# A state-space scan on one core: phase tables made on VectorE alone, and transposes of u grouped by row count

## The chip, the core and the metric

The kernel runs as one program on one core of a Trainium2 chip. Five engines work side by side, each through its own list of instructions in order: TensorE (PE, with its weight loads as PEld), VectorE (DVE), ScalarE (ACT), GpSimd (POOL) and SyncE (SP). SP, ACT and POOL also issue DMAs; a DMA that has to wait holds up whatever stands behind it on the engine that issues it. The metric is the device time of one execution in microseconds, as the median of several.

## The reference

One layer of a hybrid backbone over 2048 latent tokens and 256 context tokens of width 1024: a combined input projection, a two-dimensional neighbourhood attention (8 heads), a bidirectional diagonal state-space scan (32 groups of 16 channels, 64 complex states each), a gated merge of the two branches, and a SwiGLU feed-forward network. The part at hand is the scan:

```python
def diag_scan(lb_re, lb_im, bu_re, bu_im):
    a_re = jnp.broadcast_to(lb_re, (1, L) + lb_re.shape)
    a_im = jnp.broadcast_to(lb_im, (1, L) + lb_im.shape)
    return lax.associative_scan(_linear_combine, (a_re, a_im, bu_re, bu_im), axis=1)
...
ur, ui = drive(u_ctx)                       # context scan first
_, _, hc_re, hc_im = diag_scan(lb_re, lb_im, ur, ui)
ur, ui = drive(u_lat)                       # latent scan starts from its final state
```

Every state h obeys h[t] = lam h[t-1] + (B u)[t] with a complex lam, forwards and backwards.

## The kernel before

The kernel cuts the 2304 tokens into 288 chunks of eight. What happens within a chunk is done by matmuls; between chunks the state is multiplied by lam^8. The complex factor is split into its size, r8, and a rotation: the inputs of chunk n are turned back by n times the angle, a real scan with r8 runs over the 288 columns (`tensor_tensor_scan`), and the result is turned forward again. The cosines and sines of n times the angle, n = 0 to 287, are the phase tables `er` and `ei`, 128 x 288 each, one pair of tables for each pair of groups and each direction, 32 in all.

`s5_params` (once, before the scan) makes what the tables are built from: `eb`, the first 32 powers of the rotation for all 32 pairs, and `zz`, the powers 32, 64, 128 and 256. `s5` then runs over four quarters q of the groups, each in two sub-blocks sb, eight sub-blocks in all. A sub-block

- loads u of its four groups into `ut` (three DMAs that POOL issues, L651; the buffer is single), has ACT sort it into `un0`, `un1` (128 chunks each, latent) and `un2` (32 chunks, context) (L652),
- transposes `un` on PE (L658 to L661) into PSUM tiles `pt`, which ACT copies into `ug` (L662). `ug` holds the context columns at both ends, the latent ones between;
- builds `win` and `cl` (DVE, PE, ACT, L684 to L709) and the matrix `mt` (PE, ACT, and 16 DMAs of SP, L719 to L725),
- for each of its two pairs p and two directions d builds the phase tables (L732 to L744), drives the states with PE (`pv`, L750; one PSUM buffer), and runs the scan on DVE (L757 to L772),
- reads out with PE (`py`, L780 to L782), ACT and DVE (L784 to L788).

At the end of a quarter `yn` is transposed (L795) and stored.

The order of the instructions on every engine is set by a scheduler: it plays the program on a timeline of its own and picks the ready instruction with the highest priority. The scan has a higher priority than the input projection `in_proj` of the four token blocks b (three matmuls for each product, L92 to L94, weights through `raw` and split into `whi` by ACT, L70, and `wlo` by DVE, L71), which fills PE between the scan's matmuls. Attention (L884 to L924) follows the scan, again with what is left of `in_proj` beneath it; later the merge. While token block b = 1 is projected, `biases` (L436 to L445) builds the attention's bias tables on POOL: eight heads, each a load, four tensor operations and three stores, in the same POOL list as the loads of u.

Of the kernel before, what the change touches and what calls it, by code (L numbers as in the profile page):

```python
# [10 lines left out]
F32 = mybir.dt.float32  # L11
F32R = mybir.dt.float32r
BF16 = mybir.dt.bfloat16
AF = mybir.ActivationFunctionType
# [38 lines left out]
class Kernel:  # L53
# [394 lines left out]
    def s5_params(self, keep, tmp):  # L448
# [6 lines left out]
        def T(name, *shape):  # L455
            return (keep if name in kept else tmp).tile([P, *shape], F32, name=name)
# [136 lines left out]


        eb = T("eb", 2, 32, n)
        zz = T("zz", 4, 3, n)
        zr, zi = T("zr", n), T("zi", n)
        V.tensor_copy(zr, co[:, 1, :])
        V.tensor_copy(zi, si[:, 1, :])
# [3 lines left out]
        while m <= 256:  # L603
# [6 lines left out]
            if m < 32:  # L610
                for a0 in range(0, m, 8):
                    w = min(8, m - a0)
                    cmul(eb[:, 0, m + a0:m + a0 + w, :], eb[:, 1, m + a0:m + a0 + w, :], eb[:, 0, a0:a0 + w, :], eb[:, 1, a0:a0 + w, :],
                         zr.unsqueeze(1).to_broadcast([P, w, n]), zi.unsqueeze(1).to_broadcast([P, w, n]), (w, n))
            else:
                i = (32, 64, 128, 256).index(m)
                V.tensor_copy(zz[:, i, 0, :], zr)
                V.tensor_copy(zz[:, i, 1, :], zi)
                V.tensor_scalar(zz[:, i, 2, :], zi, -1.0, None, op0=ALU.mult)
            m *= 2  # L620
            if m <= 256:
                cmul(zr, zi, zr, zi, zr, zi, (n,))
# [6 lines left out]
    def s5(self):  # L629
        nc, I = self.nc, self.I  # L630
        V = nc.vector
        with ExitStack() as ctx:
# [7 lines left out]
            for q in range(4):  # L640
                yn = [bp.tile([P, SC, 8, 16], F32, name=f"yn{cb}") for cb in range(2)]
                for sb in range(4 // NQ):
# [10 lines left out]
                        un.append(u)  # L653
                    uc = un[2]
                    ug = bp.tile([P, NG, SEQC + NCC], F32, name="ug")
                    for g in range(NG):
                        pt = psT.tile([P, SEQC + NCC], F32, name="pt")
                        nc.tensor.transpose(pt[:, 0:NCC], uc[:NCC, g], self.ident[:NCC, :NCC])  # L658
                        for cb in range(2):
                            nc.tensor.transpose(pt[:, NCC + cb * P:NCC + cb * P + P], un[cb][:, g], self.ident)  # L660
                        nc.tensor.transpose(pt[:, SEQC:SEQC + NCC], uc[:NCC, g], self.ident[:NCC, :NCC])  # L661
                        nc.scalar.copy(ug[:, g, :], pt)  # L662


                    win = bp.tile([P, 2, NQ, 2, 2, 64], F32, name="win")
# [61 lines left out]
                    for p0 in range(0, NQ, 2):  # L727
                        hst = {}
                        for p in (p0, p0 + 1):
                            for d in range(2):  # L730
                                pr = d * 16 + pr0 + p
                                er = pp.tile([P, SEQC], F32, name="er")  # L732
                                ei = pp.tile([P, SEQC], F32, name="ei")
                                nc.scalar.copy(er[:, 0:32], self.eb[:, 0, :, pr])
                                nc.scalar.copy(ei[:, 0:32], self.eb[:, 1, :, pr])
                                for i, m in enumerate((32, 64, 128, 256)):
                                    w = min(m, SEQC - m)
                                    zr, zi, zn = (self.zz[:, i, x, pr:pr + 1] for x in range(3))
                                    ea = pp.tile([P, P], F32, name="ea", bufs=1)
                                    eb = pp.tile([P, P], F32, name="eb", bufs=1)  # L740
                                    nc.scalar.activation(ea[:, :w], er[:, 0:w], AF.Copy, scale=zr)
                                    nc.scalar.activation(eb[:, :w], ei[:, 0:w], AF.Copy, scale=zr)
                                    V.scalar_tensor_tensor(er[:, m:m + w], ei[:, 0:w], zn, ea[:, :w], op0=ALU.mult, op1=ALU.add)
                                    V.scalar_tensor_tensor(ei[:, m:m + w], er[:, 0:w], zi, eb[:, :w], op0=ALU.mult, op1=ALU.add)  # L744
                                pv = psV.tile([P, 2, 512], F32, name="pv")
                                for ri in range(2):
                                    for g2 in range(2):
# [599 lines left out]
```

## Time and profile before

| | |
|---|---|
| median of 3 runs | 3233.46 us (3233.32 to 3234.92) |
| profiled execution, its own time | 3233.39 us |
| its span, first to last instruction | 3231.6 us |
| granted TensorE clock, mean | 0.987 |
| PE busy | 97% |
| DVE, ACT, POOL busy | 73%, 49%, 28% |

The span is counted from the first instruction; 1.8 us of the execution's time lie outside it. The scan stands between about 140 and 870 us, with `in_proj` beneath it; attention and the merge follow until about 1600 us, then the feed-forward network. PE is busy nearly all the time, so what counts is PE's work, its waits, and the stretches in which its granted clock is at the lower of its two levels (0.5 of full, 1.2 GHz instead of 2.4 GHz).

### The profile page before, as it was taken

How to read it: one execution, taken by the hardware profiler on the slowest of the kernel's cores; microseconds unless marked ns; L12 is line 12 of the kernel's file. 1: busy time of each engine (PE TensorE's matmuls, PEld its weight loads, DVE VectorE, ACT ScalarE, POOL GpSimd, SP SyncE). 2: the span in 40 equal slices, each digit the busy share in tenths (PEclk: the TensorE clock that was granted, in tenths of full speed). 3: DMA queues.
4: the chain of work that ended last, by engine and by line, in shares of the span. 5: the costliest groups of instructions: out<-in, count | busy, mean ns of one | idle time of the engine just before them, and what ended most of it. 6: DMA issues, size and time to landing. Idle time of an engine off the chain costs nothing.

```text
span 3231.6 us, 54283 instructions
## 1 busy us (share of the span) xinstructions
PE 3119.2 (97%) x20600; PEld 2727.7 (84%) x20600; DVE 2348.4 (73%) x4153; ACT 1570.3 (49%) x2746; POOL 898.9 (28%) x856
## 2 busy tenths in 40 slices
PE   7999978999999998999999999999999999999998
PEld 5987766787787778788888988888989898989988
DVE  6689787897753565665657867887858966897766
ACT  4445434454355555555554444445535543554534
POOL 2000052000223232323300544742242423341243
PEclk9999989999999999999999999999999999999999
DMA  8545567454776897987847434434344434443332
GB/s 321 186 125 172 166 194 241 163 163 140 228 211 193 268 259 213 277 238 220 254 130 269 139 126 146 141 131 147 122 136 132 150 111 131 141 147 131 112 111 101
DMA packets 212853, 564.27 MB, mean 175 GB/s; under 512 B 31785, under 2 KB 63657, under 8 KB 212593
## 3 DMA queue, kind: packets, MB, share of 16 engines
q1 hardware_dynamic: 155008, 437.48, 41.2%
q0 software_dynamic: 28032, 87.64, 10.0%
q10 hardware_dynamic: 29552, 35.70, 3.2%
q8 instruction: 162, 2.65, 0.3%
q14 instruction: 99, 0.80, 0.1%
HBM read 446.95 MB, written 111.61 MB: 173 GB/s over the span
## 4 chain that ended last, share of the span: by engine, by line
PE 79%; DVE 9%; DMA 6%; issue 3%; POOL 1%; ACT 1%; SPq 0%; ACTq 0%; DVEq 0%; POOLq 0%
PE ps L92 15%; PE ps L94 15%; PE ps L93 15%; PE ps L1068 8%; PE ps L1066 8%; PE ps L1067 8%; PE o L924 3%; DVE wlo L71 3%; PE w L884 2%; PE w L905 1%; DMA raw<-in_w_qk 1%; PE pv L750 1%; PE c L886 1%; PE c L907 1%; DVE n L1130 1%
## 5 line engine op out<-in xcount | busy, mean ns | idle before, releaser
L71 DVE TENSOR_TENSOR wlo<-raw,whi 128x1024 fp32r<-128x1024 f32 (+1 forms) x522 | 688.0, 1325 | 324.6 <-ACT whi L70 323.1
L70 ACT CAST whi<-raw 128x1024 fp32r<-128x1024 f32 (+1 forms) x522 | 508.3, 976 | 519.6 <-PE ps L94 185.8
L1066 PE MATMUL ps<-X,whi 128*128 128x256 f32 x2464 | 693.4, 284 | 13.2 <-DVE u L1078 8.4
L1068 PE MATMUL ps<-X,wlo 128*128 128x256 f32 x2464 | 692.4, 284 | 11.9 <-DVE wlo L71 11.7
L1067 PE MATMUL ps<-X,whi 128*128 128x256 f32 x2464 | 689.9, 283 | 0.0
L1066 PEld LDWEIGHTS ps<-X,whi 128*128 128x128 f32 x2464 | 471.2, 191 | 17.9 <-DVE u L1078 11.7
L1068 PEld LDWEIGHTS ps<-X,wlo 128*128 128x128 f32 x2464 | 470.5, 191 | 15.1 <-DVE wlo L71 14.9
L1067 PEld LDWEIGHTS ps<-X,whi 128*128 128x128 f32 x2464 | 471.3, 191 | 0.5
L92 PE MATMUL ps<-n,whi 128*128 128x512 f32 (+1 forms) x800 | 318.2, 398 | 10.3 <-ACT t L382 6.7
L93 PE MATMUL ps<-n,whi 128*128 128x512 f32 (+1 forms) x800 | 316.7, 396 | 0.0
L94 PE MATMUL ps<-n,wlo 128*128 128x512 f32 (+1 forms) x800 | 316.3, 396 | 0.5 <-DVE wlo L71 0.5
L92 PE MATMUL ps<-whi,zh 128*128 128x512 f32 x704 | 277.1, 395 | 0.0
L94 PE MATMUL ps<-whi,zl 128*128 128x512 f32 x704 | 277.0, 394 | 0.0
L93 PE MATMUL ps<-wlo,zh 128*128 128x512 f32 x704 | 276.9, 394 | 0.0
L1049 POOL TENSOR_TENSOR os<-raw 128x512 f32<-128x512 f32 x66 | 117.4, 1780 | 406.7 <-DMA raw<-in_w_f 330.7
L70 ACT CAST whi<-os 128x1024 fp32r<-128x1024 f32 x110 | 115.5, 1050 | 204.1 <-PE ps L1067 91.7
L71 DVE TENSOR_TENSOR wlo<-os,whi 128x1024 fp32r<-128x1024 f32 x110 | 151.3, 1376 | 62.9 <-ACT whi L70 62.9
L92 PEld LDWEIGHTS ps<-n,whi 128*128 128x128 f32 x800 | 151.3, 189 | 49.6 <-ACT t L382 9.0
L93 PEld LDWEIGHTS ps<-n,whi 128*128 128x128 f32 x800 | 151.5, 189 | 35.6 <-issue 4.1
L94 PEld LDWEIGHTS ps<-n,wlo 128*128 128x128 f32 x800 | 151.3, 189 | 35.0 <-issue 1.8
L1050 POOL TENSOR_TENSOR os<-raw,os 128x512 f32<-128x512 f32 x88 | 134.0, 1523 | 150.4 <-DMA raw<-in_w_f 148.5
L92 PE MATMUL ps<-y,whi 128*128 128x512 f32 x384 | 155.5, 406 | 5.1 <-DVE t L968 1.8
(343 smaller groups left out, 7098.8 us busy)
## 6 DMA issues: line engine op xcount, KB each, us to landing
raw<-in_w_f SPq DMA_DIRECT2D x198, 512.0 KB
raw<-sums SPq DMA_DIRECT2D x66, 512.0 KB
raw<-in_w_gate SPq DMA_DIRECT2D x64, 512.0 KB
raw<-in_w_f SPq DMA_DIRECT2D x66, 256.0 KB
raw<-in_w_qk SPq DMA_DIRECT2D x32, 512.0 KB
gsc<-e ACTq DMA_DIRECT2D x64, 256.0 KB
raw<-in_w_m SPq DMA_DIRECT2D x32, 512.0 KB
t<-gsc SPq DMA_DIRECT2D x64, 256.0 KB
```

Of the source, the lines that this page charges most:

```text
L70: self.nc.scalar.copy(hi, x)
L71: self.nc.vector.tensor_tensor(lo, x, hi.bitcast(F32), op=ALU.subtract)
L92: mm(ps, l[0], r[0], start=first, stop=False)
L93: mm(ps, l[0], r[1], start=False, stop=False)
L94: mm(ps, l[1], r[0], start=False, stop=last)
L884: nc.tensor.matmul(slv, q[:, qs], kl, start=(n == 0), stop=(n == 1))
L924: nc.tensor.matmul(o[h, g, :, hf, :], l, r, start=(n == 0), stop=(n == nb + 1), skip_group_check=True)
L1049: nc.gpsimd.tensor_tensor(s24[:, 0], s13[:, 0], a11, op=ALU.subtract)
L1050: nc.gpsimd.tensor_tensor(s24[:, 1], a12, s24[:, 0], op=ALU.subtract)
L1066: mm(dst, a[0][:, k], xh, start=(first and k == 0), stop=False, skip_group_check=True)
L1067: mm(dst, a[0][:, k], xl, start=False, stop=False, skip_group_check=True)
L1068: mm(dst, a[1][:, k], xh, start=False, stop=(k == 3), skip_group_check=True)
```

## The change

Two edits in the scan, and what they need in `s5_params`.

The tables. Before, `er` and `ei` began with 32 columns copied from `eb` by ACT and were doubled four times (32, 64, 128 and the last 32 columns): each time ACT scaled the old columns by the real part of a power and DVE added the imaginary part. Now `zz` holds the nine powers 0, 32, ..., 256, and a table is the outer product of `eb` (32) and `zz` (9): two DVE multiplications of 2 x 288 elements, with the factors of `zz` repeated 32 times and those of `eb` read with a step of 32 elements, then a subtraction and an addition of 288 elements each. `ee` (both tables) keeps the buffers named `er`; `et` takes the single buffer `p1`, which the scan uses too.

The transposes. Before, each of the four groups had a PSUM tile of its own with four transposes: 32 rows, 128 rows twice, 32 rows again (the context columns stand at both ends). Now the four 32-row transposes go first into one tile and one ACT copy writes them to both ends; the eight 128-row transposes follow, two groups to a tile, and two ACT copies.

```diff
-        zz = T("zz", 4, 3, n)
+        zz = T("zz", 2, 9, n)
...
-                i = (32, 64, 128, 256).index(m)
-                V.tensor_copy(zz[:, i, 0, :], zr)
-                V.tensor_copy(zz[:, i, 1, :], zi)
-                V.tensor_scalar(zz[:, i, 2, :], zi, -1.0, None, op0=ALU.mult)
+                i = m // 32
+                w = 1 if i == 8 else i
+                cmul(zz[:, 0, i:i + w, :], zz[:, 1, i:i + w, :], zz[:, 0, 0:w, :], zz[:, 1, 0:w, :],
+                     zr.unsqueeze(1).to_broadcast([P, w, n]), zi.unsqueeze(1).to_broadcast([P, w, n]), (w, n))
...
+                    pt = psT.tile([P, NG, NCC], F32, name="pt")
                     for g in range(NG):
-                        pt = psT.tile([P, SEQC + NCC], F32, name="pt")
-                        nc.tensor.transpose(pt[:, 0:NCC], uc[:NCC, g], self.ident[:NCC, :NCC])
-                        for cb in range(2):
-                            nc.tensor.transpose(pt[:, NCC + cb * P:NCC + cb * P + P], un[cb][:, g], self.ident)
-                        nc.tensor.transpose(pt[:, SEQC:SEQC + NCC], uc[:NCC, g], self.ident[:NCC, :NCC])
-                        nc.scalar.copy(ug[:, g, :], pt)
+                        nc.tensor.transpose(pt[:, g], uc[:NCC, g], self.ident[:NCC, :NCC])
+                    ends = ug.rearrange("p g (n c) -> p g n c", c=NCC)[:, :, ::SEQC // NCC]
+                    nc.scalar.copy(ends, pt.unsqueeze(2).to_broadcast([P, NG, 2, NCC]))
+                    for g in range(0, NG, 2):
+                        pt = psT.tile([P, 2, 2, P], F32, name="pt")
+                        for j in range(2):
+                            for cb in range(2):
+                                nc.tensor.transpose(pt[:, j, cb], un[cb][:, g + j], self.ident)
+                        nc.scalar.copy(ug[:, g:g + 2, NCC:SEQC], pt.rearrange("p j c t -> p j (c t)"))
...
-                                nc.scalar.copy(er[:, 0:32], self.eb[:, 0, :, pr])
-                                nc.scalar.copy(ei[:, 0:32], self.eb[:, 1, :, pr])
-                                for i, m in enumerate((32, 64, 128, 256)):
...
-                                    nc.scalar.activation(ea[:, :w], er[:, 0:w], AF.Copy, scale=zr)
-                                    nc.scalar.activation(eb[:, :w], ei[:, 0:w], AF.Copy, scale=zr)
-                                    V.scalar_tensor_tensor(er[:, m:m + w], ei[:, 0:w], zn, ea[:, :w], op0=ALU.mult, op1=ALU.add)
-                                    V.scalar_tensor_tensor(ei[:, m:m + w], er[:, 0:w], zi, eb[:, :w], op0=ALU.mult, op1=ALU.add)
+                                low = self.eb[:, :, :, pr].unsqueeze(2).to_broadcast([P, 2, 9, 32])
+                                for x, t in enumerate((ee, et)):
+                                    z = self.zz[:, x, :, pr].unsqueeze(1).unsqueeze(3).to_broadcast([P, 2, 9, 32])
+                                    V.tensor_tensor(t.rearrange("p c (a b) -> p c a b", b=32), low, z, op=ALU.mult)
+                                V.tensor_tensor(er, er, et[:, 1], op=ALU.subtract)
+                                V.tensor_tensor(ei, ei, et[:, 0], op=ALU.add)
```

Since the scheduler plays the whole program, the order moves on every engine, well beyond the two edits. Two places are shown.

PE before, at the first sub-block of the second quarter: the transposes of one group (`un2` has 32 rows, `un0` and `un1` 128), ahead of them the last of the first quarter's `yn`, behind them `in_proj`.

```order
L795 MATMUL pt_2868<-ident_66,yn1_2115 128x128 x4
L658 MATMUL pt_2891<-ident_66,un2_2887 128x32
L660 MATMUL pt_2891<-ident_66,un0_2879 128x128
L660 MATMUL pt_2891<-ident_66,un1_2883 128x128
L661 MATMUL pt_2891<-ident_66,un2_2887 128x32
L94 MATMUL ps_6322<-n_1496,wlo_6319 128x512
```

PE of the change, at the second sub-block of that quarter: all transposes of the sub-block.

```order
L752 MATMUL pv_2862<-ug_2720,win_2739 64x288 x4
L660 MATMUL pt_2991<-ident_66,un2_2987 128x32 x4
L667 MATMUL pt_2997<-ident_66,un0_2979 128x128
L667 MATMUL pt_2997<-ident_66,un1_2983 128x128
L667 MATMUL pt_2997<-ident_66,un0_2979 128x128
L667 MATMUL pt_2997<-ident_66,un1_2983 128x128
L667 MATMUL pt_3003<-ident_66,un0_2979 128x128
L667 MATMUL pt_3003<-ident_66,un1_2983 128x128
L667 MATMUL pt_3003<-ident_66,un0_2979 128x128
L667 MATMUL pt_3003<-ident_66,un1_2983 128x128
L92 MATMUL ps_5758<-n_1495,whi_5754 128x512
```

Sixteen transposes in four mixed groups have become twelve in two runs of one row count each.

POOL before, in the bias tables (third and fourth head): the second and third load of u for the fifth sub-block, `ut_3644` and `ut_3648`, stand among the heads' operations.

```order
L442 TENSOR_TENSOR n_6596<-am_71,n_6594 128x480 x2
L651 DMA ut_3644<-us_84 128x8x64
L443 TENSOR_TENSOR n_6597<-n_6596,am_71 128x480
L436 DMA n_6605<-in_rpb 128x1x960
L443 TENSOR_TENSOR n_6597<-n_6596,am_71 128x480
L445 DMA be_83<-n_6596 128x2x320 x2
L445 DMA bi_82<-n_6597 128x2x440
L651 DMA ut_3648<-us_84 32x8x64
L442 TENSOR_TENSOR n_6607<-am_71,n_6605 128x480 x2
```

POOL of the change, at the start of the bias tables: `ut_3282`, `ut_3286` and `ut_3290` are the fifth sub-block's three loads, `ut_3552` the sixth's first.

```order
L653 DMA ut_3282<-us_84 128x8x64
L653 DMA ut_3286<-us_84 128x8x64
L653 DMA ut_3290<-us_84 32x8x64
L436 DMA n_5838<-in_rpb 128x1x960
L653 DMA ut_3552<-us_84 128x8x64
L442 TENSOR_TENSOR n_5840<-am_71,n_5838 128x480 x2
L443 TENSOR_TENSOR n_5841<-n_5840,am_71 128x480
L436 DMA n_5849<-in_rpb 128x1x960
```

All three loads of the fifth sub-block have moved ahead of the first head; the sixth's other two stand behind the last head, where they stood before as well.

## Rows read from the trace of the kernel before

**Rows 1.** The page's first part: busy time, share of the span, instructions.
```profile
PE 3119.2 (97%) x20600; PEld 2727.7 (84%) x20600; DVE 2348.4 (73%) x4153; ACT 1570.3 (49%) x2746; POOL 898.9 (28%) x856
```

**Rows 2.** Windows: length, busy PE, PEld, DVE, ACT, POOL, granted clock, DMA share, GB/s.
```profile
185.00:392.00 207.00, 207.00 (x1217) 167.00 (x1216) 176.45 (x376) 101.96 (x225) 7.10 (x9) 1.00 0.49 151
392.00:548.00 156.00, 128.84 (x670) 103.57 (x669) 130.77 (x224) 59.08 (x121) 65.20 (x67) 0.91 0.71 217
548.00:870.00 322.00, 321.66 (x1733) 254.53 (x1732) 269.53 (x535) 152.98 (x312) 17.65 (x30) 1.00 0.52 170
870.00:1040.00 170.00, 165.21 (x996) 136.16 (x996) 75.66 (x175) 84.37 (x151) 46.17 (x77) 0.98 0.71 212
1040.00:1420.00 380.00, 356.70 (x2414) 297.08 (x2412) 237.90 (x536) 197.37 (x350) 108.06 (x180) 0.97 0.88 257
```

**Rows 3.** Waits of PE from 392 to 548 us: total, times, longest.
```profile
PE pv L750 <- DVE p L758: 9.0, 2, 7.2
PE ps L92 <- ACT t L382: 5.4, 2, 4.7
PE pv L750 <- ACT win L695: 4.6, 1, 4.6
...
PE py L780 <- issue: 3.4, 1, 3.4
```

**Rows 4.** Timeline of POOL, 441 to 451 us: start, length, instruction.
```profile
444.16 0.92 POOL L651 DMA_DIRECT2D ut<-us  x1
...
449.88 0.61 POOL L651 DMA_DIRECT2D ut<-us  x1
```

**Rows 5.** Timeline of ACT, 447 to 459 us; in brackets the idle time before.
```profile
447.77 0.62 ACT L652 COPY un<-ut 128x512 f32<-128x512 f32 x1 [10.55 <-DMA ut<-us]
...
458.85 0.62 ACT L652 COPY un<-ut 32x512 f32<-32x512 f32 x1 [7.47 <-DMA ut<-us]
```

**Rows 6.** Timeline of DVE at 449 us.
```profile
448.95 0.69 DVE L398 SCALAR_TENSOR_TENSOR qt<-t,qt 128x512 fp32r<-128x512 f32 x1 [8.82 <-ACT qt L397]
```

**Rows 7.** Windows over two stretches at the lower clock.
```profile
447.50:454.30 6.80, 3.18 (x13) 1.91 (x14) 5.35 (x10) 3.57 (x6) 2.99 (x5) 0.50 0.87 252
464.30:467.70 3.40, 3.27 (x13) 1.94 (x14) 3.40 (x11) 1.47 (x4) 0.20 (x1) 0.53 1.00 203
```

**Rows 8.** Timeline of PE: a mixed group of transposes; a run of eight; in_proj.
```profile
422.34 0.24 PE L658 MATMUL pt<-ident,un 32*128 32x32 f32 x1
...
423.06 0.33 PE L694 MATMUL pt<-ident,Lr 128*128 128x128 f32 x1
...
328.67 1.04 PE L795 MATMUL pt<-ident,yn 128*128 128x128 f32 x8
329.46 0.48 PE L93 MATMUL ps<-n,whi 128*128 128x512 f32 x1
...
402.26 0.40 PE L92 MATMUL ps<-n,whi 128*128 128x512 f32 x1
402.50 0.39 PE L93 MATMUL ps<-n,whi 128*128 128x512 f32 x1
```

**Rows 9.** Groups by line: busy us, mean ns; idle before, releaser.
```profile
L741 ACT ACTIVATE ea<-er,zz 128x32 f32<-128x32 f32 (+2 forms) x128 | 44.4, 347 | 85.8 <-DVE er L743 78.2 <-DMA vs<-e 4.3 <-DVE ei L744 1.5
L742 ACT ACTIVATE eb<-ei,zz 128x32 f32<-128x32 f32 (+2 forms) x128 | 43.6, 340 | 24.7 <-DVE ei L744 20.0 <-DMA vs<-e 2.9 <-DVE p L765 0.9
L744 DVE SCALAR_TENSOR_TENSOR ei<-er,zz,eb 128x32 f32<-128x32 f32 (+2 forms) x128 | 38.1, 297 | 0.2
L743 DVE SCALAR_TENSOR_TENSOR er<-ei,zz,ea 128x32 f32<-128x32 f32 (+2 forms) x128 | 37.0, 289 | 1.4 <-ACT ea L741 0.4
L757 DVE TENSOR_TENSOR p<-pv,er 128x576 f32<-128x576 f32 x32 | 24.1, 753 | 1.8 <-PE pv L750 1.5
L799 DVE SCALAR_TENSOR_TENSOR yt<-pt,yt 128x512 fp32r<-128x512 f32 x16 | 19.5, 1245 | 8.3 <-ACT yt L798 8.2
L759 DVE TENSOR_TENSOR v<-p,p 128x288 f32<-128x288 f32 x32 | 14.5, 452 | 0.1
```

More of the change, by code (lines that the diff above doesn't have):

```diff
@@ L595, in s5_params @@
         eb = T("eb", 2, 32, n)
-        zz = T("zz", 4, 3, n)
+        zz = T("zz", 2, 9, n)
+        V.memset(zz[:, 0, 0, :], 1.0)
+        V.memset(zz[:, 1, 0, :], 0.0)
         zr, zi = T("zr", n), T("zi", n)
@@ L731, in s5 @@
                                 pr = d * 16 + pr0 + p
-                                er = pp.tile([P, SEQC], F32, name="er")
-                                ei = pp.tile([P, SEQC], F32, name="ei")
-                                nc.scalar.copy(er[:, 0:32], self.eb[:, 0, :, pr])
-                                nc.scalar.copy(ei[:, 0:32], self.eb[:, 1, :, pr])
-                                for i, m in enumerate((32, 64, 128, 256)):
[L737 to L740, printed above, removed]
-                                    nc.scalar.activation(ea[:, :w], er[:, 0:w], AF.Copy, scale=zr)
-                                    nc.scalar.activation(eb[:, :w], ei[:, 0:w], AF.Copy, scale=zr)
-                                    V.scalar_tensor_tensor(er[:, m:m + w], ei[:, 0:w], zn, ea[:, :w], op0=ALU.mult, op1=ALU.add)
-                                    V.scalar_tensor_tensor(ei[:, m:m + w], er[:, 0:w], zi, eb[:, :w], op0=ALU.mult, op1=ALU.add)
+                                ee = pp.tile([P, 2, SEQC], F32, name="er")
+                                et = pp.tile([P, 2, SEQC], F32, name="p1", bufs=1)
+                                er, ei = ee[:, 0], ee[:, 1]
+                                low = self.eb[:, :, :, pr].unsqueeze(2).to_broadcast([P, 2, 9, 32])
[4 more added lines that the diff above has]
+                                V.tensor_tensor(ei, ei, et[:, 0], op=ALU.add)
                                 pv = psV.tile([P, 2, 512], F32, name="pv")
```

## Prediction

> **What bounds the kernel now.** I read the page's busy times first, then the kernel cut into stages, then the waits of the stage that stood out, then the timelines of the engines in that chain.
>
> PE is busy 97% of the span, DVE 73%, ACT 49% [rows 1]. So work taken from ACT or DVE is worth nothing by itself; it counts where PE waits for it. The stages say where [rows 2]: from 185 to 392 and from 548 to 870 us, PE has no idle time worth naming (207.00 of 207, 321.66 of 322) and the clock is full. Between them, from 392 to 548, it is busy for 128.84 of 156 us at a mean granted clock of 0.91. POOL works 65.20 us there, against 7.10 and 17.65 in the stages beside it: this is where the bias tables are built. So the scan's stage has 27.2 us of idle PE and a slower clock, all in one place, and elsewhere only PE's own work counts.
>
> The waits of that place [rows 3]: the longest sum is `pv` waiting for DVE's read of the one `pv` buffer, 9.0 us in two waits. The timelines show what stood behind it. ACT waited 10.55 us and 7.47 us for loads of u [rows 5]; POOL had issued these two loads at 444.16 and 449.88, between operations of the bias heads [rows 4]. As ACT works in order, the rope's scaling (L397) behind the first of them came late, DVE waited 8.82 us for that [rows 6], and PE for DVE. The reader is to see a DMA in the wrong place of POOL's list reach PE by way of two engines. Behind each wait stands a stretch at 0.50 and 0.53 of the clock, the lower of the two levels (1.2 GHz) [rows 7].
>
> **The transposes of u.** Here PE's own work changes, where PE does not wait. A mixed group of four runs from 422.34 to 423.06, so 0.72 us; eight transposes of 128 rows in a run take from 328.67 to 329.46, 0.10 us each [rows 8]. A sub-block had four such groups, 2.88 us. Now it has eight large ones, 0.79, and four small ones that I price like large ones, 0.40. The excess of the mixed group over four of a run is 0.72 - 0.40 = 0.32 us, and the row count changes four times in it (the matmuls around it have 128 rows), so 0.08 for a change; the new order has two, 0.16. That is 1.35 us, 1.53 less, and over eight sub-blocks 12 us. If instead the price hung on the instruction (0.18 each, mixed or not), only the four that are gone would count, 0.72 x 8 = 6 us; if a change cost nothing in the new order, 14. I take 12, since the run of eight is the nearest row.
>
> **The loads of u.** The change leaves these lines alone, but the order moves: the fifth sub-block's three loads now stand ahead of the first bias head. In ACT's new order the three copies of them stand ahead of the first copy of block 1's keys (`t1`, L382), so that ACT has them behind it when the rope work starts. What goes: the 9.0 us of `pv` waits [rows 3]; the lower clock behind them, half of PE's busy 3.18 and 3.27 us, so 3.2 [rows 7]; and half of the 3.4 us that `py` waited afterwards [rows 3], as `mt` was late by the same chain but SP's slow DMAs had a part in it. Sum 14 us. The lower bound is 0: something else may be last in the same place, since the 5.4 us on ACT's copy `t` and the 4.6 us on `win` [rows 3] are not of this chain, and I leave both as they are. The upper bound is the stage's whole loss, 27.2 us of idle plus 0.09 of 156 us of clock, 41. The sixth sub-block's second load stands behind the last head. The heads fill most of the stage of 156 us; in the new order the copy that needs this load stands on ACT behind the second quarter's first transposes of `yn`, which by the order's rows at the prices above lie some 130 us of PE's work behind the first head. It may just be late, and this belongs to the lower bound.
>
> **The tables.** ACT loses 44.4 + 43.6 us of scaling [rows 9] and 64 small copies of `eb`; its copies of `ug` change from 32 to 24 and cost about the same. All of it lies beside PE: 0 us. DVE loses 38.1 + 37.0 = 75.1 us [rows 9] and gains 32 times two multiplications of 576 elements and two of 288. By L757 (753 ns for 576) and L759 (452 for 288) [rows 9] this is 32 x 2.41 = 77 us, so no change; I see no reason for less than some 70. But `eb` is read with a step of 32 elements, and no row reads so. L799, which steps by eight elements, takes 1245 ns for 512, while L757's pace makes 670 of that [rows 9]. At L799's pace the multiplication of 576 takes 1.40 us, a table 3.70, and DVE works 118 us, 43 more. I take this dear value, as the nearest row. What hides it: DVE is busy 176.45 + 130.77 + 269.53 = 577 of the 685 us of the scan [rows 2], and the new order spreads the scan over more PE work. Counting the rows of `in_proj` between the first transposes of u and the last of `yn`, 584 triples of width 512 and 251 of width 256 have become 651 and 304. At 0.24 us for a matmul of 512 [rows 8] and half for 256 that is 48 + 19 = 67 us more PE work beneath the same scan. So the 43 us have a cover of 67, and I count 0. If the cover is gone, it is up to 43.
>
> The Trainium skill, in "SBUF — State Buffer", section "Door 1: The DMA port swizzle", speaks against the change here: SBUF is read in lines of 16 bytes, and an access that goes to a new line each time pays for it. L799 agrees in kind, and no run here shows the new read itself. By that rule every multiplication takes the dear value, which is what the fourth rival below needs; without it that rival falls away.
>
> `s5_params` gains 28 small DVE operations and loses 12, once, ahead of the scan, while PE still projects u: 0.
>
> **What comes later.** The 67 us that move under the scan are missing under attention: behind the scan's end the triples fall from 160 wide and 53 narrow to 101 and none. Attention with `in_proj` beneath it (870 to 1040) leaves PE idle for 4.8 of 170 us; without it (1040 to 1420) for 23.3 of 380, and the DMA share is 0.88 there [rows 2]. In proportion, 60 us moved from the first kind to the second cost 60 x (6.1% - 2.8%) = 2 us. I take 6, since attention's first steps now follow more closely on one another with loads of their own; bounds 0 and 25 (a hole of a tenth in some 250 us).
>
> **The sum.** -12 - 14 + 0 + 6 = -20. Made against the profiled execution, 3233.4 us (its span and 1.8 us around it), which stands 0.1 us below the median of the runs, this gives 3213 us.
>
> **Rivals.** First, the wait is replaced: the rope's scaling, the stores of k, or the sixth sub-block's late load end last in the bias stage, and only the transposes pay: -12 + 6, so 3227 us. For it: three other waits in rows 3; against it: none is queued behind a load of u.
>
> Second, the bias stage is calm: with ACT's load gone and loads early, all 41 us go: -12 - 41 + 6, 3186 us. Against it speak the bias operations on POOL, which stay.
>
> Third, attention starves: PE's filler is gone too soon and the later stage takes 25 us: -12 - 14 + 25, so 3232 us, no change. For it: the DMA share of 0.88; against it: the merge's matmuls fill in as before.
>
> Fourth, and slower: DVE becomes the scan's bound. Its place is the `pv` row on PE, which waits until DVE has read the single `pv` buffer; the dear multiplications make every table 1.3 us later, and the single `p1` holds the table back until the scan before is done with it. It decides from the point where DVE's share passes what it has now without a PE wait, 176.45 of 207, 85% [rows 2]: the cover of 67 us brings DVE work of its own (`wlo`), and 43 us then come through on PE almost whole. With 38 of them: -12 - 14 + 6 + 38, so 3251 us. For it: 85% busy already; against it: the spread order.
>
> **How the numbers follow.** Chances: the forecast 0.45, the wait replaced 0.20, the calm stage 0.10, attention starved 0.13, DVE the bound 0.12. No change means within 0.2%, 6.5 us, which is about what a measurement of this kernel can tell. Faster by more: nearly all of the forecast's share (0.43), half of the first rival (0.10, it stands at the edge), the calm stage (0.10), a little of the third: 0.65. Same: the other half of the first and most of the third, 0.18. Slower: the fourth and a rest of the third, with the reordered attention and merge as a risk that I can't price: 0.17. The likeliest case alone runs from 3200 to 3226; the range from 3190 to 3243 leaves out half of the calm stage and most of the fourth rival.
>
> **What would show it.** Right: PE's transposes of `un` in runs, 0.10 us from one to the next; no wait of ACT for u in the bias stage; in that stage less than 18 us of PE idle time; DVE's multiplication of 576 elements at 0.75 or 1.40 us, and no PE wait on `pv` outside the bias stage in either case. Wrong: PE waits on `pv` spread over all four quarters (fourth rival), new waits of `o` or `w` right behind `in_proj`'s end (third), or ACT idle before a copy of `un` during the sixth sub-block (first).

## The result: slower by one per cent, and the profile after

The changed kernel takes 3266.35 us (median of 4 runs, 3262.95 to 3270.11), the kernel before 3233.39 in the same comparison (4 runs, 3224.34 to 3234.92). The ratio, an estimate from all runs and so not quite the quotient of the medians, is 1.0107, with a 95% interval from 1.0093 to 1.0122. The forecast of 3213 us and its range up to 3243 both missed. The profiled execution of the changed kernel took 3270.11 us, its span is 3268.3.

The page's busy times after (before: [rows 1]):

```profile
span 3268.3 us, 53697 instructions
PE 3121.9 (96%) x20568; PEld 2734.0 (84%) x20568; DVE 2409.5 (74%) x4043; ACT 1489.0 (46%) x2418; POOL 907.5 (28%) x856
```

PE works 2.7 us more than before although its transposes got cheaper, and the span is 36.7 us longer. So 34 us are new idle time of PE, and PE's gain has been eaten by something else.

The stages of the prediction in the windows after (columns: stretch, its length, busy time and instructions of each engine, granted clock, DMA share, GB/s), to be held against [rows 2]:

```profile
185.00:392.00 207.00, 204.95 (x1203) 168.24 (x1203) 187.47 (x317) 73.00 (x110) 9.28 (x12) 1.00 0.52 164
392.00:548.00 156.00, 124.39 (x638) 100.96 (x637) 139.13 (x189) 37.31 (x55) 65.25 (x64) 0.88 0.66 204
548.00:870.00 322.00, 319.94 (x1772) 259.27 (x1771) 285.40 (x470) 118.87 (x172) 8.01 (x11) 1.00 0.51 165
1040.00:1420.00 380.00, 335.60 (x2241) 274.92 (x2240) 222.83 (x517) 189.44 (x342) 107.69 (x178) 0.95 0.81 236
```

The scan outside the bias stage is almost as full as before (3.8 us more idle time in its 529 us). The bias stage has not become better: 31.6 us idle against 27.2. The loss stands in attention: 44.4 us idle in 380 against 23.3, at a clock of 0.95 against 0.97.

The two kernels no longer reach the same place at the same time, so the next windows go by the program's own marks: the ends of the scan's four quarters (last transposes of `yn`), the end of `in_proj`, the last `o` of attention. First, of L92 alone, which is a third of `in_proj`'s matmuls in these stretches (columns: stretch, length, PE busy and count, PEld, clock, DMA share, GB/s). The kernel before:

```profile
187.00:342.00 155.00, 77.45 (x228) 42.75 (x228) 1.00 0.51 156
342.00:549.00 207.00, 83.22 (x219) 43.30 (x219) 0.93 0.64 198
549.00:722.00 173.00, 81.89 (x225) 42.20 (x225) 1.00 0.52 172
722.00:868.00 146.00, 63.99 (x163) 30.63 (x163) 1.00 0.51 164
868.00:1063.00 195.00, 80.44 (x213) 41.26 (x213) 0.98 0.74 222
```

The changed kernel:

```profile
183.00:353.00 170.00, 86.54 (x250) 46.91 (x250) 1.00 0.50 154
353.00:574.00 221.00, 90.94 (x236) 47.06 (x236) 0.92 0.64 201
574.00:754.00 180.00, 87.61 (x239) 44.90 (x239) 1.00 0.54 174
754.00:926.00 172.00, 84.37 (x231) 43.35 (x231) 1.00 0.53 168
926.00:1031.00 105.00, 41.12 (x101) 19.45 (x100) 0.97 0.71 224
```

Every quarter of the scan carries more of `in_proj` and is longer: by 15, 14, 7 and 26 us. Behind the scan's end 101 of these matmuls are left instead of 213. Then attention alone, all engines, before and after:

```profile
1063.00:1695.00 632.00, 607.31 (x4322) 514.60 (x4321) 384.82 (x887) 347.57 (x652) 164.54 (x270) 0.98 0.79 231
```

```profile
1031.00:1732.00 701.00, 655.39 (x4633) 550.39 (x4632) 405.84 (x958) 381.62 (x716) 191.66 (x317) 0.97 0.76 225
```

Without `in_proj` beneath it attention runs 69 us longer and leaves PE idle for 45.6 us instead of 24.7. The first 129 us behind `in_proj`'s end, before and after, show where:

```profile
1063.00:1192.00 129.00, 121.02 (x749) 96.14 (x747) 85.24 (x190) 65.63 (x113) 34.19 (x57) 0.99 0.89 262
```

```profile
1031.00:1160.00 129.00, 99.93 (x616) 77.83 (x615) 57.22 (x156) 61.96 (x117) 42.46 (x72) 0.87 0.75 214
```

All of the 20.9 us more stand in this stretch (29.1 us idle against 8.0), and the clock falls from 0.99 to 0.87. PE's waits in the changed kernel, from 1028 to 1420 us (columns: engine, its row, what it waited for, us in total, times, longest):

```profile
PE w L907 <- ACT s L900: 14.9, 8, 2.9
PE ps L92 <- DVE t L970: 8.3, 3, 4.7
PE ps L92 <- DMA y<-as: 7.4, 3, 5.0
```

Of these, 13.6 us of `w` and 7.0 us of the loads `y<-as` fall into the stretch from 1031 to 1160. With 4.3 us in which `o` waited for ACT's `pl` and 4.2 us for the loads `y<-ys` they make up its 29.1 us. The waits for DVE's `t` come later.

The account of the span, from PE's rows and the clock's records: idle time rises by 8.7 us in the scan, 20.9 in attention and 6.8 in the merge, and falls by 2.4 elsewhere: 34.0. PE's busy time rises by 2.7, which is what two terms make together. The transposes give 12.0 back. The clock stands 42.7 us longer at the lower of its two levels; PE was busy in 29.6 us of these, and at half the clock half of that, 14.8 us, is lost.

### The profile page after: what moved, and what is told of

The parts are those of the page before. It is cut to its first block, busy times and chain, and to the rows that moved or that the text cites. A ratio compares the mean times of both kernels' runs of the same rounds, so it can differ in the third digit from the quotient of the medians.

```text
span 3268.3 us, 53697 instructions
## 1 busy us (share of the span) xinstructions
PE 3121.9 (96%) x20568; PEld 2734.0 (84%) x20568; DVE 2409.5 (74%) x4043; ACT 1489.0 (46%) x2418; POOL 907.5 (28%) x856
## 4 chain that ended last, share of the span: by engine, by line
PE 71%; DVE 10%; DMA 8%; issue 3%; POOL 2%; ACT 1%; SPq 0%; DVEq 0%; POOLq 0%; ACTq 0%
PE ps L92 13%; PE ps L93 13%; PE ps L94 13%; PE ps L1070 8%; PE ps L1068 8%; PE ps L1069 8%; DVE wlo L71 3%; PE o L926 3%; DMA n<-in_rpb 2%; PE w L886 2%; PE w L907 1%; DMA raw<-in_w_ba 1%; PE c L888 1%; PE c L909 1%; PE pv L752 1%
## 5 line engine op out<-in xcount | busy, mean ns | idle before, releaser
L1068 PEld LDWEIGHTS ps<-X,whi 128*128 128x128 f32 x2464 | 473.0, 192 | 14.8 <-DVE u L1080 9.7
L92 PE MATMUL ps<-n,whi 128*128 128x512 f32 (+1 forms) x800 | 318.9, 399 | 21.0 <-ACT e L426 16.7
L92 PE MATMUL ps<-whi,zh 128*128 128x512 f32 x704 | 277.1, 395 | 0.0
L92 PEld LDWEIGHTS ps<-n,whi 128*128 128x128 f32 x800 | 152.4, 190 | 57.8 <-ACT e L426 17.6
L92 PE MATMUL ps<-y,whi 128*128 128x512 f32 x384 | 159.3, 415 | 29.1 <-DVE t L970 12.6
```

The costliest lines, as they stand in the source:

```text
L92: mm(ps, l[0], r[0], start=first, stop=False)
L1068: mm(dst, a[0][:, k], xh, start=(first and k == 0), stop=False, skip_group_check=True)
```

## The experiments

Four theories are named in the expectations. A: the new tables make the order draw the scan out; `in_proj` moves under the scan, attention loses its filler and waits. B: the strided multiplications make VectorE the bound. C: chance waits in the bias stage eat the gains. D, formed later: the scan on the chip really is longer through VectorE's added work, and `in_proj` only fills the hole. All times are medians with their range; all ratios are to the kernel before on the same chip.

**The two parts by themselves.** `transposes_only` has the new transposes and the old tables, `tables_only` the reverse.

> The kernel before with the new transposes alone, the tables as before. Theory A (the new tables draw the scan out in the scheduler's order, so more of in_proj lies under the scan and less under attention, which then waits): here the order leaves 153 us of in_proj's PE work behind the scan, against 131 in the kernel before and 71 in the changed one. The changed kernel lost 33 us net of 12 us that its transposes save, so 45 us for 60 us of moved work, 0.75 us for one; this one gains 12 + 22 x 0.75, so about 3205 us, faster. Theory B (the multiplications with a step of 32 elements make VectorE the bound): no tables, so only the transposes count, 3221 us. Theory C (a chance wait in the bias stage): 3221 us or worse, by what the new order draws there.

> The changed kernel with the transposes as before, so the new tables alone. Theory A: the order leaves 64 us of in_proj's work behind the scan, 67 less than in the kernel before: 3233 + 67 x 0.75 = 3283 us, with the waits of PE under attention as in the changed kernel. Theory B: the same tables, 12 us of transposes more than the changed kernel, 3278 us, with waits on pv in the scan. Theory C: the loads of u stand between the bias heads again as in the kernel before; if the wait of the changed kernel there was chance, 3245 to 3255 us.

Measured: 3230.58 us (3224.89 to 3240.35), 0.9993 [0.9978, 1.0008], and 3259.52 (3251.80 to 3262.78), 1.0073 [1.0056, 1.0089]. The tables lose by themselves; the transposes change nothing that can be told. A's prices missed both (3205 and 3283 us), B's and C's figures for the tables missed too; only C's "3221 or worse" for the transposes fits. The largest waits in the scan of `transposes_only`, of PE and of SP's queue:

```profile
PE ps L92 <- ACT e L426: 22.3, 2, 21.9
SPq L357 <- DMA n<-in_rpb: 25.1, 1, 25.1
```

PE is busy 13.9 us less than before (3105.3 us against 3119.2) and idle 13.6 us more, and one wait of 21.9 us is the largest of the new ones: SP stood for 25.1 us before a load of the next block's `n`, whose ring buffer a bias head still held, with `w_gate`'s weights queued behind it. This is theory C's mechanism.

**The price on VectorE.** `own_et` puts `et` into the two buffers of `v` instead of the single `p1`; `contig` lays `eb` out so that the multiplications read with step 1.

```diff
-  et = pp.tile([P, 2, SEQC], F32, name="p1", bufs=1)
+  et = pp.tile([P, 2, SEQC], F32, name="v")                  # own_et
...
-  eb = T("eb", 2, 32, n)
+  self.ebt = T("eb", 2, n, 32)                               # contig
+  eb = self.ebt.rearrange("p c n a -> p c a n")
...
-  low = self.eb[:, :, :, pr].unsqueeze(2).to_broadcast([P, 2, 9, 32])
+  low = self.ebt[:, :, pr, :].unsqueeze(2).to_broadcast([P, 2, 9, 32])
```

> The changed kernel, but et takes its buffer from the two of v and not the single p1 of the scan, so a table need not wait for the scan before it. The multiplications cost the same. Theory A: the order leaves 104 us of in_proj's work behind the scan: 3233 - 12 + 27 x 0.75 = 3241 us. Theory B: VectorE has the same work, so 3266 us as in the changed kernel. Theory C: anything between, by the waits of its bias stage.

> The changed kernel, but eb is kept with the 32 powers of a pair side by side, so that the multiplications read it with a step of one element. The order of the instructions is that of the changed kernel as far as the counts of in_proj tell. The multiplication should fall from 1.22 us to 0.75 us, 30 us of VectorE's work over 64 of them. Theory A: 3266 us, within 6, since the order decides. Theory B: 30 us less, 3236 us. Theory C: 3266 us with the same 12 us wait in the bias stage.

Measured: `own_et` 3259.86 us (3255.08 to 3261.84), 1.0075 [1.0060, 1.0090]; `contig` 3258.97 (3252.18 to 3266.35), 1.0077 [1.0059, 1.0094]. The multiplication in the groups by line (columns: line, engine, operation, tile, shapes, count, then busy us and mean ns), the changed kernel first, and in `contig` by the tile `er` (ns least/median/most):

```profile
L744 DVE TENSOR_TENSOR er<-eb,zz 128x576 f32<-128x576 f32 x32 | 39.4, 1233 | 0.9
```

```profile
L745 DVE TENSOR_TENSOR er<-eb,zz x32: 750/758/760, 173.0 to 862.7; 128x576 f32<-128x576 f32 x32
```

The step costs 0.47 us a multiplication, 30 us in all. Taking it away gives back 0.30% of the 1.07, so B explains about a third; `own_et` gives back 0.32%. Of the forecasts, A's 3241 us and B's 3266 missed for `own_et`, B's 3236 for `contig`, and A's 3266 "within 6" by a little.

**Both together, and the bias stage.** `own_contig` has both edits. The `_split` versions build four bias heads in the second token block and four in the third instead of all eight in the second:

```diff
-            if b == 1:
-                self.biases(ring)
+            if b in (1, 2):
+                self.biases(ring, range((b - 1) * 4, b * 4))
```

> The changed kernel with both costs of the tables taken away: eb laid out so that the multiplications read with step 1, and et in the buffers v in place of the single p1. By the order 104 us of in_proj stand behind the scan's end. Theory B (DVE's strided reads and the shared buffer bound the scan): both gone, 3225 to 3235 us. Theory A: half of the filler is back, attention's idle time about 40 us, 3245 to 3255 us; each of the two alone gave 3259.

> The kernel before, with the bias tables of four heads made beside token block 1 and of the other four beside block 2, in place of all eight beside block 1. Theory C (the chain of eight heads, some 130 us long on POOL and its DMAs, sets when block 2's tokens can be loaded, and SP holds the gate's weights back behind that load): two chains of half the length let PE pass; of the 27 us of idle PE and 27 us of lower clock between the first head and the scan's end some 15 us go, 3218 us. Theory A: the order leaves 134 us of in_proj behind the scan, 131 before, so no change from there: 3232 us. Without theory C: 3232 us.

> The new transposes alone, with the bias tables split over blocks 1 and 2. In the kernel with the new transposes alone one wait of 21.9 us stood in the bias stage, with 34 us at the lower clock between the first head and the scan's end, and its 12 us of saved work did not show. Theory C: this wait goes, and the saved work shows: 3231 - 20 to 30, about 3205 us. If the 12 us are given back elsewhere (attention or the merge): 3225 us or more.

> The changed kernel with the bias tables split over blocks 1 and 2. Theory C as the main cause of the loss: the 12.3 us wait and the clock behind it go, and the kernel comes below 3233 us. Theory A as the main cause: attention still has only 71 us of in_proj beneath it and keeps its 45 us of idle PE, so only some 15 us are gained, about 3248 us, still slower than before.

> own_contig with the bias heads spread over the second and third token block (four each). Theory C for what is left over (the bias stage's idle time, 37 us in own_contig against 25 in before): the idle time there falls to about 24 and the time to 3230 to 3240 us. If the rest is something else, it stays at 3243 to 3250.

Measured: `own_contig` 3246.07 us (3236.84 to 3253.61), 1.0039 [1.0026, 1.0053]; `before_split` 3225.95 (3217.90 to 3230.59), 0.9972 [0.9959, 0.9984]; `transposes_split` 3239.04 (3234.45 to 3244.82), 1.0016 [1.0006, 1.0025]; `after_split` 3263.83 (3257.35 to 3270.05), 1.0096 [1.0080, 1.0111]; `own_contig_split` 3247.84 (3243.87 to 3251.15), 1.0039 [1.0026, 1.0053]. Spreading the heads helps the old kernel, which so becomes the fastest version of all, faster than both kernels compared here, with a time between C's 3218 and A's 3232. It does not rescue the changed one, and it gives `own_contig` nothing. C says where the transposes' gain went in one version, not why the change loses: its forecasts for `transposes_split` and `after_split` (about 3205, below 3233) both missed, and `after_split` is slower than A's 3248 too.

`own_contig` came out where A had it (3245 to 3255), not B. With the changed kernel, `own_et` and `contig` it makes a table of four, all with the new transposes: 1.07% lost with both costs of the tables, 0.75 without the shared `p1`, 0.77 without the step, 0.39 without either. Each edit is worth 0.3 to 0.4%, with the other or without. The step does this with the filler unmoved: `after` and `contig` both leave 101 of the L92 matmuls behind the scan, `own_et` and `own_contig` 147 and 148.

**The filler moved by other means.** `before_er1` is the kernel before with one buffer instead of two for `er` and for `ei`: no new operation, but the tables wait for each other. `before_dve` is the kernel before with three maxima of 288 elements behind each table, each of a table with itself, which change no value.

```diff
+  for x in (er, ei, er):                                     # before_dve
+      V.tensor_tensor(x, x, x, op=ALU.max)
```

> The kernel before with one change of size: the phase tables er and ei have one buffer each and not two. No multiplication with a step, the same operations, but the scheduler must draw the scan out: 48 us of in_proj's work are left behind it, against 131. Theory A (what counts is the cover that attention loses): the kernels with 64 and 71 us left lost some 26 us against before for 60 to 67 us moved, 0.4 us for one, so 83 x 0.4 = 33 us here, 3266 us, with 45 us or more of idle PE in attention. Theory B (the dear multiplications): there are none, 3233 us. Theory C (the bias stage alone): 3233 us, up or down by its waits there.

> The kernel before, old tables and old transposes, with three further VectorE operations of 288 elements behind each of the 32 tables (a maximum of the table with itself, which changes no value): 32 x 3 x about 0.45 us = 43 us of VectorE work and nothing else. By the order 71 us of in_proj stand behind the scan's end, as in the changed kernel. Theory D (VectorE's time bounds the scan; in_proj that moves under it is not cover but borrowed, and is paid back in attention): slower by 0.8 to 1.3 %, 3258 to 3275 us, with attention's idle time at 40 to 50 us. Theory A' (not VectorE's work, but the changed structure of the tables and buffers): within 0.4 %, 3228 to 3246 us. If VectorE's work were truly covered, as the prediction had it: within 0.2 %.

Measured: 3285.11 us (3284.90 to 3285.87), 1.0162 [1.0147, 1.0177], and 3265.49 (3260.74 to 3270.92), 1.0097 [1.0080, 1.0115]. The last quarter and what is behind it in `before_er1`, L92 alone as above, then the whole stretch from the scan's end to attention's last `o` and its two largest waits:

```profile
765.00:950.00 185.00, 90.33 (x245) 45.99 (x245) 1.00 0.52 164
950.00:1001.00 51.00, 23.40 (x59) 11.08 (x59) 1.00 0.86 269
```

```profile
950.00:1729.00 779.00, 713.40 (x4943) 598.28 (x4942) 428.87 (x1032) 412.20 (x777) 222.16 (x367) 0.95 0.76 222
```

```profile
PE w L905 <- ACT s L898: 32.3, 14, 4.0
PE ps L92 <- DMA y<-as: 22.0, 7, 6.4
```

With 59 instead of 213 left behind the scan, attention is idle for 65.6 us at a clock of 0.95: the same loss, larger (A had 3266 us), with nothing of the change in it. `before_dve` leaves 71 us of `in_proj` behind by the order, just what the change leaves, and loses what the change loses; time and attention's idle time (47.0 us) are as D had them. But it adds VectorE's work as well as moving the filler, so it fits A and D alike. `cheap_tables_only` tells more: `own_contig`'s tables, nearly as cheap for VectorE as the old ones (81 us measured against 75), with the old transposes.

> own_contig with the old transposes: the tables as outer products, read with step 1 and with et in v, 76 us of VectorE work against 75 before; by the order 84 us of in_proj behind the scan's end. If the rest of own_contig's loss (0.39 %) comes from the transposes' new order: within 0.2 % of before. If it comes from the tables (one chain on VectorE without ACT's part, er taking longer to come free): 0.3 to 0.6 % slower, like own_contig; then the transposes give nothing and cost nothing, as alone.

Measured: 3272.52 us (3265.84 to 3274.34), 1.0105 [1.0088, 1.0122]. Its multiplication, L92 in the last quarter and behind the scan, and attention alone:

```profile
L741 DVE TENSOR_TENSOR er<-eb,zz 128x576 f32<-128x576 f32 x32 | 24.3, 758 | 0.9
```

```profile
747.00:919.00 172.00, 82.33 (x226) 42.38 (x226) 1.00 0.52 162
919.00:1044.00 125.00, 48.94 (x120) 23.12 (x119) 0.97 0.70 221
```

```profile
1044.00:1732.00 688.00, 639.96 (x4540) 538.92 (x4539) 400.13 (x943) 370.62 (x701) 182.51 (x299) 0.97 0.75 223
```

The multiplications take 0.76 us, and the loss is as large as with the dear ones. The filler has moved all the same (120 behind), and attention is idle for 48.0 us. Neither forecast (at most 0.6%) came true. VectorE's dear price is not needed for the loss; the moved filler is there in each of the versions so far that lose a per cent. But the same tables with the new transposes lose only 0.39% (`own_contig`): the two differ by 21 us where the transposes save 12, so one version alone is weak evidence here.

**The filler held back.** In the `_held` versions the last block's projection waits for a value (a zero) that VectorE writes in the scan's last sub-block:

```diff
+  if (q, sb, p, d) == (3, 1, 1, 0):                          # in s5, behind the scan's two operations
+      V.tensor_scalar(self.held, v[:, 0, 0:1], 0.0, None, op0=ALU.mult)
...
+  if b == 3:                                                 # in in_proj
+      V.tensor_tensor(nt[0][:, 1, 0:1], nt[0][:, 1, 0:1].bitcast(F32), self.held, op=ALU.add)
```

> The changed kernel, with the last token block's input projection held back: its first operand waits for a value that VectorE writes in the last sub-block of the scan (the value is zero, so nothing is left out). By the order 128 us of in_proj then stand behind the scan's end, as before the change (131), against 71 in the changed kernel. Theory A (the lost filler makes attention wait, and that is the loss): PE's idle time from the scan's end to attention's last o goes from 50 us back to about 30, PE is not idle beneath the scan's last quarter, and the time is 3225 to 3240 us. Rival D (the new tables make the scan itself longer, in_proj only fills the hole): PE is idle for 40 us or more beneath the last quarter, the scan ends no more than 20 us earlier, and the time is 3260 to 3285 us.

> own_contig with the last block's input projection held back as in after_held: 131 us of in_proj behind the scan's end, the same as before the change. Theory A: attention's idle time about 30 us and 3215 to 3235 us, below after_held, since nothing of the dear tables is left. Rival D: the scan is shorter than in after_held, so PE is idle for less than 20 us under its last quarter, and the time is 3235 to 3250 us. If the time stays at 3255 or above with 131 us behind, the filler's amount is not the cause and A falls.

> own_contig_split with the last block's input projection held back to the scan's last sub-block (127 us behind the scan's end by the order). Theory D: the scan is about as long as before, so the hold costs and gains little: within 0.2 % of own_contig_split. With the 12 us of the transposes on top it would be 3215 to 3230 us and beat the kernel before; a chance of one in three for that.

> cheap_tables_only with the last block's input projection held back to the scan's last sub-block, as in after_held: 128 us of in_proj behind the scan's end by the order, VectorE's work as before the change. Theory A (the order: filler taken from attention without need): attention's idle time back to 25 to 32 us, the scan ends about as in the kernel before (868 to 880 us), no idle PE of more than 10 us in its last quarter, 3230 to 3243 us. If the tables cost the scan something on the chip even so: the scan's last quarter idles for 20 us or more and the time stays above 3255.

> before_dve with the same hold: 131 us of in_proj behind the scan's end, 45 us of VectorE work added. Theory D (VectorE's added time is real on the chip): PE idles for 20 to 40 us in the scan's last quarter and the time stays at 3255 to 3270. Theory A alone (only the order costs): 3230 to 3243 us as in cheap_held.

Measured: `after_held` 3266.55 us (3265.36 to 3267.83), 1.0105 [1.0083, 1.0126]; `own_contig_held` 3243.81 (3237.41 to 3248.39), 1.0034 [1.0022, 1.0046]; `own_contig_split_held` 3240.85 (3236.26 to 3244.55), 1.0021 [1.0011, 1.0032]; `cheap_held` 3264.59 (3258.58 to 3270.59), 1.0092 [1.0079, 1.0105]; `before_dve_held` 3275.06 (3270.26 to 3278.28), 1.0124 [1.0109, 1.0140]. The scan's last quarter and attention alone in `after_held`:

```profile
753.00:896.00 143.00, 122.93 (x650) 96.07 (x649) 128.57 (x214) 43.66 (x66) 13.83 (x26) 0.89 0.42 136
1085.00:1728.00 643.00, 616.89 (x4333) 522.44 (x4334) 386.78 (x892) 350.83 (x659) 163.88 (x270) 0.98 0.77 229
```

and the last quarter in `cheap_held`, with its largest wait:

```profile
750.00:902.00 152.00, 136.57 (x697) 105.27 (x696) 121.67 (x213) 46.86 (x72) 13.78 (x25) 0.91 0.43 140
```

```profile
PE pv L752 <- DVE p L760: 7.0, 2, 6.4
```

Attention gets its filler back and is as good as before (26.1 us idle in `after_held`, 20.1 in `cheap_held`), as A said. But the time stays, as A did not say; its forecasts missed for all of these kernels that had one from it. Now the scan's last quarter is idle for 20.1 and 15.4 us, at a clock of 0.89 and 0.91. The first three quarters have already taken their larger share, so whatever is kept for attention is missing at the scan's end. PE's largest wait there is for VectorE's reads of `pv` (5.4 and 7.0 us), at DVE shares of 90% and 80%. D's times came for `after_held` and `own_contig_held`, and not for `before_dve_held`; its sign for `after_held`, 40 us of idle PE in the last quarter, came only by half, and with cheap tables nearly as much. `own_contig_split_held` stays within 0.2% of `own_contig_split`, as forecast.

L92 in the four quarters of `cheap_held`, to be held against the kernel before:

```profile
184.00:349.00 165.00, 82.64 (x239) 45.01 (x239) 1.00 0.50 154
349.00:572.00 223.00, 91.45 (x239) 47.16 (x239) 0.93 0.62 198
572.00:750.00 178.00, 86.23 (x233) 43.77 (x233) 1.00 0.53 173
750.00:902.00 152.00, 54.74 (x141) 27.22 (x141) 0.91 0.43 140
```

Over the whole scan that is about the filler of the kernel before (852 against 835; 853 in `after_held`, 836 in `before_dve_held`), and yet the scan takes 37 us longer than its 681 us (31 and 38 in the other two). These kernels lose 31, 34 and 42 us. So moved filler and a starved attention are not the whole cause: with attention's filler given back, the loss stands in a longer scan. Whether the scan is longer because the filler lies unevenly in it, too much early and too little at the end, or because the tables themselves take longer on the chip, these runs can't tell apart.

What stays open is therefore whether the new tables would cost anything if each sub-block carried exactly the `in_proj` that it carried before. No version reached that. Nor is it settled why the transposes' 12 us never show. Against the version that differs in them alone they give nothing in the kernel before (0.9993), lose with the spread heads (1.0016 against 0.9972) and with the dear tables (1.0107 against 1.0073), and gain with the cheap tables (1.0039 against 1.0105). Each time the order of the whole program moves too. PE saves 12 us, 0.37%, each time; what is left when that is taken off runs from 0.3% faster to 0.8% slower.

## Why the prediction was wrong, point by point

**The transposes: right, and worth nothing.** In the first sub-block of the changed kernel (timeline of PE; start, duration, instruction, count):

```profile
199.19 0.43 PE L660 MATMUL pt<-ident,un 32*128 32x32 f32 x4
199.55 0.50 PE L93 MATMUL ps<-n,whi 128*128 128x512 f32 x1
199.88 0.39 PE L94 MATMUL ps<-n,wlo 128*128 128x512 f32 x1
200.12 0.60 PE L667 MATMUL pt<-ident,un 128*128 128x128 f32 x4
200.47 0.48 PE L92 MATMUL ps<-n,whi 128*128 128x512 f32 x1
200.79 0.39 PE L93 MATMUL ps<-n,whi 128*128 128x512 f32 x1
```

Four small transposes take 0.36 us from the first to the next instruction, four large ones 0.35. Over the scan the transposes of `un` take 21.9 us before, from one start to the next, and 9.9 after: the 12 us of the sum. The size was right. That the row count is what is paid for is not shown by itself: behind the four large transposes, where no row count changes, the next matmul also takes 0.32 us to the one after it (200.47 to 200.79), against 0.24 elsewhere (199.88 to 200.12).

**The loads of u: the first rival.** In the bias stage the waits for u are gone, as forecast, and others replaced them. The largest waits of the bias stage after (392 to 548 us), of PE, ACT and SP's queue, for [rows 3]:

```profile
PE ps L92 <- ACT e L426: 12.3, 1, 12.3
PE ps L92 <- ACT t L382: 6.7, 2, 4.5
PE pv L752 <- DVE strip L729: 3.9, 1, 3.9
```

```profile
529.63 1.04 ACT L70 CAST whi<-raw 128x1024 fp32r<-128x1024 f32 x1 [18.47 <-DMA raw<-in_w_gate]
```

```profile
SPq L357 <- DMA n<-in_rpb: 16.7, 1, 16.7
```

SP waits 16.7 us for a ring buffer that a bias head holds; its loads of `w_gate` come behind that, ACT waits 18.47 us for one, and PE 12.3. The prediction had looked at POOL's list and at ACT's, and not at what SP's list holds behind a load that needs a buffer. The stage is 4.4 us worse instead of 14 better. The first rival's 0 was nearer than the forecast's 14, but neither its candidates (the rope's scaling, the stores of k, a late load of u) nor its sign came: for the sixth sub-block ACT waited at most 1.4 us for u.

**The tables: the price right, the cover wrong.** A multiplication takes 1.23 us, between the two bounds of 0.75 and 1.40 and nearer to the dear one. In the Trainium skill, "SBUF — State Buffer", "Door 1: The DMA port swizzle", says that each access that crosses to a new line of 16 bytes pays a penalty. The traces agree: 1.23 us with the step, 0.76 us with step 1. As the forecast said, PE hardly waited for `pv` in the scan (4.2 us in five waits for DVE's reads). But that was bought with 67 us of `in_proj`, which the prediction counted as a cover that costs nothing here. And the cover is not the whole price: `contig`, with the same filler under the scan, is 0.30% faster than the changed kernel, so the dear reads did not come at 0 but at some 10 us.

**What comes later: the step that failed.** It is the same 67 us, priced at +6 from attention's mean idle share. Attention alone lost 20.9 us by idle time and another 8 by the clock (41.0 us at the lower level against 20.5, of which PE was busy in 32.7 and 16.8), and the merge 6.8 and 1.2: some 37 where the bounds ended at 25. The third rival named this place. The mean failed because the loss is not spread: it stands in the first 129 us in which attention runs alone, now at an earlier step of attention than before. There `w` waits for ACT's `s`, the merge's first matmuls for loads of `y`, `o` for ACT's `pl`, and the mean granted clock is 0.87. This is where the 37 us stand in the changed kernel; the held versions do not bear out that they go when attention gets its filler back. There the time is lost in the scan instead, and why the scan is longer stays open.

**The sum of the rivals.** The fourth rival, VectorE as the bound, had the nearest time (3251), but that was luck: by its own sign, waits of `pv` spread over all quarters, it did not happen. What happened is nearest to the first and the third together, the third larger than its bound: -12 + 37 + 4 for the bias stage is +29. The two profiled executions lie 36.7 us apart (the medians 33); the rest is 4 us more idle time in the scan's other stages and some 5 us lost to the clock behind the merge, less small gains.

## What to carry to other kernels

Work that fills one stage's waits is a fixed amount: what a new order moves under an earlier stage is not cover but a loan, and the later stage pays it back with its waits and its clock. Price it at the waits that it used to stand in front of, not at a mean. Holding it back at the end does not undo the loan: here the time was then lost in the scan. And where one order is made for the whole program, a saving of 0.4% must be tried in several surroundings, since the new order alone moves the time by as much.

## What was not expected of the hardware

A VectorE multiplication of 576 fp32 elements that reads one input with a step of 128 bytes takes 1.23 us, against 0.76 with step 1: 63% more, though only one of its two inputs has the step at every element. A mixed group of transposes costs PE 0.18 us an instruction [rows 8], against 0.09 in a run of four; put down to the changes of row count alone, that is an estimate of 0.08 to 0.09 us for each. And idle time mostly came with a lower clock, as in [rows 7]: 20.9 us more of it in attention went with 20.5 us more at the lower level of 1.2 GHz. But not in a fixed ratio: `before_dve` is idle for 33 us more than the kernel before (145.4 against 112.4), with only 2 us more at the lower level.
